# The splits of five token sums moved to later places in the order of ScalarE and VectorE

## The chip, the cores and the metric

The kernel runs on one core of a Trainium2 chip. The metric is the device time of one execution in microseconds (us): the median of several runs. TensorE (PE) does the matmuls, VectorE (DVE) and ScalarE (ACT) split operands and empty PSUM, GpSimd (POOL) adds, SyncE (SP) issues the DMAs.

## The reference

One encoder layer is applied to a prompt of 256 tokens and to a sample of 2048 tokens, both 1024 wide, in float32. What matters here is the first step, the projection of the normalised tokens by one weight matrix of 1024 x 3072:

```python
h = rms_norm(x, g_pre)
proj = h @ w_in
q, k, v, z_a, u_f, z_f = jnp.split(proj, [...], axis=-1)
y_a = neighbourhood_attention(q, k, v, rpb)
y_f = fourier_mix(u_f, w_fourier, b_fourier)
mixed = jnp.concatenate([rms_norm(y_a, g_na) * jax.nn.silu(z_a),
                         rms_norm(y_f, g_f) * jax.nn.silu(z_f)], axis=-1)
return x + rms_norm(mixed @ w_out, g_post)
```

## The kernel before, in words

**Three matmuls for one.** A float32 operand is held as two parts: a high part (a rounded copy, made by ScalarE) and a remainder (operand minus high part, made by VectorE). A product is high x high + high x remainder + remainder x high, so `mm3` (lines 170 to 173) issues three matmuls for each piece: L171, L172, L173. A product cannot pass its second or third matmul before the remainders are there.

**The prompt's stage** (lines 743 to 781) makes 16 blocks of the prompt's projections, numbered `b`. A block is 24 matmuls of 256 columns. `b_raw(b + 2)` (line 574) splits the weights of the block after next: ScalarE's cast `wh` (L577), VectorE's remainder `wl` (L578). ScalarE empties the block (L777) and SP stores it (L779, L781). Beside that, the stage makes work for the next one: `n_scale` scales the sample's tokens on VectorE (L416), `n_sum` forms sums and differences of token blocks on VectorE (L439, at b = 8 to 11), and `n_first(j)` (line 441) splits the j-th of seven such token operands: one ScalarE cast `xh` of 128 x 2048 (L444), one VectorE remainder `xl` of 128 x 2048 (L445). `op_split` (line 482) splits the weight operands `vh`, `vl` (L493, L494, for operand 5 L489, L490) in two halves each.

**The stage after it**, `vu(0, range(2, 4), hooks)` (lines 500 to 536, called in line 808), makes v and u of half of the sample's tokens by a scheme in which seven products of sums stand for eight. Its sequence has 14 steps, called products here, numbered i from 0: token operand 0 in steps 0 and 1, operand 1 in 2 and 3, and so on to operand 6 in 12 and 13. A product is 12 matmuls of 512 columns. At step i, before the matmuls, come in this order: loads of weight sums (`op_load`, SP), splits of weight sums (`op_split`: operand 2 at i = 2, 3 at 4, 4 at 6, 5 at 8, 6 at 10), and the functions hooked to i in the order in which they were hooked. Hooked are `n_first`, `rows_load(5)` to `rows_load(8)` (SP, line 298, at i = 1, 3, 5, 7; 1024 KB each, called xm5 to xm8 here), `rows_square` of these (ScalarE, two L305 activations with accumulators, at i = 4, 6, 8, 10), and from i = 8 on the first weights of the next stage (`w_load`, `w_sums`, `a_split`: L562, L563). After the matmuls of a product VectorE adds it up (L521; in products 0 and 1 ScalarE copies it, L524), and SP stores the finished ones (L364).

**What sets the order.** All engines but the DMA rings run in the order in which the code is written; no scheduler moves anything. Tiles of 8 KB a partition (`xh`, `xl`, `xm`, the sums) share 16 buffers, so a load waits for the last reader of the buffer that it gets.

Of the kernel before, what the change touches and what calls it, by code (L numbers as in the profile page):

```python
# [169 lines left out]
def mm3(nc, out, lh, ll, rh, rl, first, last):  # L170
    nc.tensor.matmul(out, lh, rh, start=first, stop=False)  # L171
    nc.tensor.matmul(out, lh, rl, start=False, stop=False)  # L172
    nc.tensor.matmul(out, ll, rh, start=False, stop=last)  # L173


def build(tc, A, O):
# [46 lines left out]
    def mmt(n):  # L223
        x = mmc[0] % 5 > 2
        mmc[0] += 1
        return ps.tile([128, n], F32, tag="t" if x else "a", name="mm", bufs=2 if x else 3)
# [21 lines left out]
    def k8(dtype, name, shape=(128, 4, 512)):  # L248
        return hp.tile(list(shape), dtype, tag="k8", name=name, bufs=NK)
# [151 lines left out]
    def n_load(x):  # L401
        if type(x) is tuple:
            nq[x] = k8(F32, "nx")
            nc.sync.dma_start(nq[x], A["xq"][0, x[0], x[1]])
            return
        nx = [k8(F32, "nx") for kh in range(2)]
        for kh in range(2):
            for b in range(2):
                nq[x, kh, b] = nx[kh][:, 2 * b:2 * b + 2]
                nc.sync.dma_start(nq[x, kh, b], A["xq"][1, kh, b][:, 2 * x:2 * x + 2])  # L410

    def n_scale(x, kh, b, ks=range(4)):
        v_ = nq[kh, b] if x is None else nq[x, kh, b]
        for k in ks if x is None else range(2):
            kk = 4 * kh + 2 * (x or 0) + k
            nc.vector.scalar_tensor_tensor(out=v_[:, k], in0=v_[:, k], scalar=gpre[:, kk:kk + 1],  # L416
                                           in1=ivp[int(x is not None)][b], op0=ALU.mult, op1=ALU.mult)
# [16 lines left out]
    def n_sum(x):  # L434
        if x == 0:
            nq["t3"] = k8(F32, "nt")
        o, i0, i1, op = (("t3", (1, 1), (0, 1), ALU.subtract), ((0, 1), (0, 1), (0, 0), ALU.subtract),
                         ((0, 0), "t3", (0, 0), ALU.add), ((1, 0), (0, 0), (1, 0), ALU.subtract))[x]
        nc.vector.tensor_tensor(out=nq[o], in0=nq[i0], in1=nq[i1], op=op)  # L439

    def n_first(j):
        src = nq[((0, 0), (1, 0), (0, 0), (0, 1), "t3", (1, 0), (1, 1))[j]]
        h, l = bnew[0, j] = [k8(F32R, "x" + x) for x in "hl"]
        nc.scalar.copy(h, src)  # L444
        nc.vector.tensor_tensor(out=l, in0=src, in1=f_(h), op=ALU.subtract)  # L445
# [27 lines left out]
    def op_load(j):  # L473
        if j < 2:
            l = [load(US, A["wv"][j][:, 2 * x:2 * x + 2], "vr") for x in range(2)]
        else:
            l = [gt(US, F32R, "vl") for x in range(2)]
            for x in range(2):
                nc.sync.dma_start(f_(l[x]), sD[(3, 2, 1, 0, 4)[j - 2]][:, 2 * x:2 * x + 2])
        op_[j] = [None, l]  # L480

    def op_split(j):
        r = op_[j][1]
        h = op_[j][0] = [gt(US, F32R, "vh"), hp.tile([128, 2, 512], F32R, tag="vw", name="vh", bufs=3)]
        l = op_[j][1] = [gt(US, F32R, "vl") for x in range(2)] if j < 2 else r
        for x in range(2):
            src = r[x] if j < 2 else f_(r[x])
            if j == 5:
                nc.scalar.activation(h[x], src, AF.Copy, scale=-1.0)  # L489
                nc.vector.scalar_tensor_tensor(out=l[x], in0=src, scalar=-1.0, in1=f_(h[x]), op0=ALU.mult,  # L490
                                               op1=ALU.subtract)
            else:
                nc.scalar.copy(h[x], src)  # L493
                nc.vector.tensor_tensor(out=l[x], in0=src, in1=f_(h[x]), op=ALU.subtract)  # L494
# [79 lines left out]
    def b_raw(b):  # L574
        wh, wl = [gt(BS, F32R, "w" + x) for x in "hl"]
        src = wp_[b]
        nc.scalar.copy(wh, src)  # L577
        nc.vector.tensor_tensor(out=wl, in0=src, in1=wh.bitcast(F32), op=ALU.subtract)  # L578
        wb[b] = wh, wl
# [106 lines left out]
    def wz_load(n):  # L686
        for x in range(n):
            wp_.append(load(BS, A["wz"][len(wp_)], "wr"))
# [54 lines left out]
    for b in range(16):  # L743
        kind, blk = divmod(b, 4)
        if b < 10:
            wz_load(1)
        if b in (0, 2):
            n_load((b // 2, 1))
        if b == 10:
            op_load(0)  # L750
        if b == 12:
            op_load(1)
        if b < 14:
            b_raw(b + 2)
        if b < 8:
            x, y = divmod(b, 2)
            n_scale(None, *divmod(x, 2)[::-1], range(2 * y, 2 * y + 2))
        elif b < 12:
            n_sum(b - 8)
        if b in (3, 5, 12, 13):  # L760
            n_first((3, 5, 12, 13).index(b))
        if b > 13:
            op_split(b - 14)
        p = mmt(512)[:, :TP]
        wh, wl = wb.pop(b)
        for k in range(KC):
            mm3(nc, p, wh[:, k], wl[:, k], hp_[:, k], lp_[:, k], k == 0, k == KC - 1)
        o = st.tile([128, 256], F32, tag="f", name="f", bufs=3)
        if kind == 1:
            v = [(o, p)]  # L770
        elif kind == 3:
            v = [(o[:, 128 * x:128 * x + 128].rearrange("p (x r c) -> p r x c", x=2, c=16),
                  p[:, 128 * x:128 * x + 128].rearrange("p (r x c) -> p r x c", x=2, c=16)) for x in range(2)]
        else:
            v = [(o.rearrange("p (r b c) -> p b r c", b=2, c=32), p.rearrange("p (b r c) -> p b r c", b=2, c=32))]
        for d, i in v:
            nc.scalar.activation(d, i, AF.Silu if kind < 2 else AF.Copy, scale=-0.125 if kind == 3 else 1.0)  # L777
        if kind < 2:
            nc.sync.dma_start(zD[kind, blk * 128:blk * 128 + 128, :TP], o)  # L779
        else:  # L780
            nc.sync.dma_start((kD if kind == 2 else qD)[blk, :, :TP], o)  # L781

    def call(f, *a):
        return lambda: f(*a)
# [11 lines left out]
    def at(i, f, *a):  # L796
        hooks.setdefault(i, []).append(call(f, *a))

    for x in range(4, 7):
        at(3 * x - 12, n_first, x)  # L800
    for x in range(4):
        at(2 * x + 1, rows_load, x + 5)
        at(2 * x + 4, rows_square, x + 5)
# [19 lines left out]
    for i in range(16):  # L823
# [48 lines left out]
        for j in range(7):  # L872
# [28 lines left out]
            if sg == 0:  # L901
                x, y = divmod(7 * (pr - 1) + j, 14)
# [19 lines left out]
            for f, d in ((u_load, 0), (u_split, 3), (u_stage1, 5)):  # L922
                x = 7 * pr + j - 7 - d
# [649 lines left out]
    for k in range(2, len(G) + 2):  # L1573
# [17 lines left out]
        x = k // 2  # L1591
# [68 lines left out]
        if 32 <= k < 36:  # L1660
            x, d = k - 32, atiles[k - 32]
# [126 lines left out]
```

## Time and profile before

| | |
|---|---|
| median of 3 runs | 938.73 us (937.64 to 939.05) |
| the profiled execution's own time | 937.48 us |
| its span, first to last instruction | 935.7 us |
| TensorE busy | 925.3 us, 99% |
| VectorE busy | 669.9 us, 72% |
| ScalarE busy | 469.8 us, 50% |
| granted TensorE clock | 0.999 |

The profiled execution took 937.48 us, of which 935.7 us lie between its first and its last instruction; all times below that are not a median are counted from the span's start. In the timeline's rows stand the start, the duration, the engine (a q behind it: its queue, for DMA issues), the line, the operation, the tiles written and read, the shape and how many were merged into the row; idle time of the engine ahead of it and what ended it stand in square brackets. A row that merges several starts with the first and ends with the last. Consecutive instructions of VectorE or ScalarE overlap by about 0.09 us, so the step from start to start says what one costs in a series.

### The profile page before, as it was taken

The page shows a single profiled execution, that of the slowest core. Times are in us where ns is not written, and L with a number is a line of the kernel's source. Part 1 is how long each engine was busy: PE and PEld are TensorE (multiplying, and loading weights), DVE is VectorE, ACT ScalarE, POOL GpSimd, SP SyncE. Part 2 cuts the span into 40 slices and gives each one's busy share as a digit, 9 for nine tenths or more (in the row PEclk, how much of TensorE's full clock was granted, in tenths as well). Part 3 has the DMA queues.
Part 4 walks back from the last instruction along what each step waited for, and adds up shares of the span by engine and source line. Part 5 has one row for each costly group of instructions (what it writes and reads, how often), then busy time and mean ns, then how long its engine had stood idle before and what let it go on. Part 6 is the DMA issues. An engine that isn't in the chain of part 4 may idle for free.

```text
span 935.7 us, 18895 instructions
## 1 busy us (share of the span) xinstructions
PE 925.3 (99%) x6790; PEld 774.5 (83%) x6790; DVE 669.9 (72%) x1308; ACT 469.8 (50%) x1038; POOL 332.0 (35%) x337
## 2 busy tenths in 40 slices
PE   9999999999999999999999999999999999999997
PEld 7889988888888888888888888978788887888886
DVE  6487997688864967597666645677665666659997
ACT  5856577623332743233334425667655666654443
POOL 3200002436650300363333200445456565525444
PEclk9999999999999999999999999999999999999999
DMA  9899777468573999758888789888779899879993
GB/s 323 329 360 400 217 253 281 158 246 314 201 288 151 352 400 359 265 209 316 294 310 286 273 287 309 295 262 257 245 248 274 264 300 283 255 237 377 341 340 128
DMA packets 144829, 264.04 MB, mean 282 GB/s; under 512 B 21784, under 2 KB 84632, under 8 KB 141984
## 3 DMA queue, kind: packets, MB, share of 16 engines
q1 hardware_dynamic: 144576, 262.81, 80.9%
q8 instruction: 54, 0.88, 0.4%
q14 instruction: 39, 0.32, 0.1%
q10 hardware_dynamic: 160, 0.02, 0.0%
HBM read 174.75 MB, written 95.35 MB: 289 GB/s over the span
## 4 chain that ended last, share of the span: by engine, by line
PE 94%; DMA 3%; DVE 2%; issue 1%; ACT 0%; DVEq 0%; SPq 0%
PE mm L172 18%; PE mm L173 18%; PE mm L171 17%; PE ptb L1425 10%; PE po L1425 10%; PE pv L1508 5%; PE ptb L1485 3%; PE s L1179 3%; PE pab L1005 2%; PE ptb L1179 2%; DMA woD<-wo 1%; PE py L171 1%; PE py L173 1%; PE py L172 1%; PE pf L1425 1%
## 5 line engine op out<-in xcount | busy, mean ns | idle before, releaser
L171 PE MATMUL mm<-xh,wa 128*128 128x512 f32 x448 | 174.4, 389 | 0.0
L173 PE MATMUL mm<-xh,wa 128*128 128x512 f32 x448 | 174.3, 389 | 0.0
L172 PE MATMUL mm<-xl,wa 128*128 128x512 f32 x448 | 174.3, 389 | 0.0
L548 POOL TENSOR_TENSOR ws<-wr 128x512 f32<-128x512 f32 x16 | 22.2, 1386 | 259.3 <-DMA wr<-wz 246.2
L171 PEld LDWEIGHTS mm<-xh,wa 128*128 128x128 f32 x448 | 84.1, 188 | 17.5
L173 PEld LDWEIGHTS mm<-xh,wa 128*128 128x128 f32 x448 | 84.1, 188 | 17.4
L172 PEld LDWEIGHTS mm<-xl,wa 128*128 128x128 f32 x448 | 84.1, 188 | 17.4
L1425 PE MATMUL po<-w,yh 128*128 128x512 f32 x280 | 86.8, 391 | 0.0
L1425 PE MATMUL ptb<-wo,yh 128*128 128x512 f32 x272 | 86.7, 400 | 0.0
L1213 POOL TENSOR_SCALAR w<-w,m 128x352 f32<-128x352 f32 (+4 forms) x136 | 75.4, 572 | 30.4 <-PE s L1179 14.0
L563 DVE TENSOR_TENSOR wa<-wr,wa 128x512 fp32r<-128x512 f32 x60 | 57.7, 969 | 30.6 <-ACT wa L562 30.3
L1206 ACT ACTIVATE w<-w,m 128x352 f32<-128x352 f32 (+4 forms) x136 | 69.9, 521 | 12.5 <-DVE m L1201 12.1
L861 DVE TENSOR_TENSOR f<-u,mm 128x512 f32<-128x512 f32 x64 | 43.6, 681 | 34.1 <-PE mm L173 29.5
L172 PE MATMUL mm<-vl,xh 128*128 128x512 f32 x168 | 65.6, 390 | 0.4 <-DVE vl L494 0.4
L171 PE MATMUL mm<-vh,xh 128*128 128x512 f32 x168 | 65.4, 389 | 0.0
L173 PE MATMUL mm<-vh,xl 128*128 128x512 f32 x168 | 65.4, 389 | 0.0
L1425 PEld LDWEIGHTS ptb<-wo,yh 128*128 128x128 f32 x272 | 49.3, 188 | 14.8 <-ACT sqa L1536 3.4
L1425 PEld LDWEIGHTS po<-w,yh 128*128 128x128 f32 x280 | 52.3, 188 | 11.0
L562 ACT CAST wa<-wr 128x512 fp32r<-128x512 f32 x60 | 36.5, 617 | 42.7 <-PE mm L173 16.8
L1508 PEld LDWEIGHTS pv<-pt,v 96*64 96x64 f32 (+2 forms) x1280 | 45.2, 137 | 11.6 <-issue 6.6
L1425 PE MATMUL po<-w,yl 128*128 128x512 f32 x140 | 54.5, 389 | 0.0
L1425 PE MATMUL ptb<-wo,yl 128*128 128x512 f32 x136 | 53.1, 391 | 0.0
(249 smaller groups left out, 2192.3 us busy)
## 6 DMA issues: line engine op xcount, KB each, us to landing
wr<-wz SPq DMA_DIRECT2D x48, 512.0 KB
vl<-sD SPq DMA_DIRECT2D x20, 512.0 KB
xm<-xm SPq DMA_DIRECT2D x9, 1024.0 KB
oD<-ofs SPq DMA_DIRECT2D x18, 512.0 KB
of<-oD SPq DMA_DIRECT2D x18, 512.0 KB
yr<-yD SPq DMA_DIRECT2D x34, 256.0 KB
zD<-f SPq DMA_DIRECT2D x16, 512.0 KB
woD<-wo SPq DMA_DIRECT2D x16, 512.0 KB
```

The lines of the kernel that those rows point to most:

```text
L171: nc.tensor.matmul(out, lh, rh, start=first, stop=False)
L172: nc.tensor.matmul(out, lh, rl, start=False, stop=False)
L173: nc.tensor.matmul(out, ll, rh, start=False, stop=last)
L562: nc.scalar.copy(o[:, 0], src)
L563: nc.vector.tensor_tensor(out=o[:, 1], in0=src, in1=o[:, 0].bitcast(F32), op=ALU.subtract)
L861: nc.vector.tensor_tensor(out=dst(f, b), in0=src(uu[u]), in1=src(p), op=op)
L1179: nc.tensor.matmul(sp[2 * b + h][64 * y:64 * y + 64, j * w:(j + n) * w], g["q"][hs, 128 * b + 64 * y:128 * b + 64 * y + 64], kk[hs, k:k + ...
L1206: nc.scalar.activation(w, w, AF.Exp, bias=m[:, h:h + 1], scale=-1.0, accum_out=m[:, 2 + h:3 + h])
L1213: nc.gpsimd.tensor_scalar(w, w, m[:, 4 + h:5 + h], 1.0, ALU.mult, ALU.mult)
L1425: nc.tensor.matmul(p, (d["l"] if x == 2 else d["h"])[:, c], w(n, int(x == 1), c), start=j == 0, stop=j == 11)
L1485: nc.tensor.transpose(ptb[2 * b + y][:nk, x:x + 64], g["w"][b][ys, h, c0:c0 + nk], ident[ys, ys])
L1508: nc.tensor.matmul(p[hs, b, o], v[:nk, b, x, hs], g["pt"][b][:nk, h, j * 128 + o.start:j * 128 + o.stop], start=first, stop=last)
```

## The change

Two lists of numbers that set when `n_first` is called are changed; nothing else:

```diff
@@ in the loop over b @@
-        if b in (3, 5, 12, 13):
-            n_first((3, 5, 12, 13).index(b))
+        if b in (3, 5, 13):
+            n_first((3, 5, 13).index(b))
@@ ahead of vu(0, ...) @@
-    for x in range(4, 7):
-        at(3 * x - 12, n_first, x)
+    for x in range(3, 7):
+        at(3 * x - 8 if x > 3 else 1, n_first, x)
```

Operand 2 is split at b = 13 instead of 12, operand 3 at product 1 instead of b = 13, operands 4, 5 and 6 at products 4, 7 and 10 instead of 0, 3 and 6. Each keeps its cast on ScalarE and its remainder on VectorE. The instructions of TensorE, GpSimd and SP stand as before; some of the shared buffers change hands.

In the rows below, names carry the number of the tile in the program. The remainders `xl` of operands 2 to 6 are xl_1193, xl_1230, xl_1345, xl_1407 and xl_1481 before, and xl_1226, xl_1356, xl_1431, xl_1494 and xl_1567 now; `wl` are the remainders of a block's weights (the last three belong to blocks 13, 14 and 15), `vl` those of weight sums, two for an operand.

VectorE before, from block 11 to the start of the products:

```order
L578 TENSOR_TENSOR wl_1152<-wr_1007,wh_1151 128x1024
L439 TENSOR_TENSOR nx_677<-nx_594,nx_677 128x2048
L578 TENSOR_TENSOR wl_1189<-wr_1043,wh_1188 128x1024
L445 TENSOR_TENSOR xl_1193<-nx_594,xh_1192 128x2048
L578 TENSOR_TENSOR wl_1226<-wr_1079,wh_1225 128x1024
L445 TENSOR_TENSOR xl_1230<-nx_745,xh_1229 128x2048
L494 TENSOR_TENSOR vl_1264<-vr_1114,vh_1262 128x1024
L494 TENSOR_TENSOR vl_1265<-vr_1116,vh_1263 128x1024
L494 TENSOR_TENSOR vl_1301<-vr_1184,vh_1299 128x1024
L494 TENSOR_TENSOR vl_1302<-vr_1186,vh_1300 128x1024
L445 TENSOR_TENSOR xl_1345<-nt_1049,xh_1344 128x2048
```

The same stretch of VectorE now:

```order
L578 TENSOR_TENSOR wl_1152<-wr_1007,wh_1151 128x1024
L439 TENSOR_TENSOR nx_677<-nx_594,nx_677 128x2048
L578 TENSOR_TENSOR wl_1189<-wr_1043,wh_1188 128x1024
L578 TENSOR_TENSOR wl_1222<-wr_1079,wh_1221 128x1024
L445 TENSOR_TENSOR xl_1226<-nx_594,xh_1225 128x2048
L494 TENSOR_TENSOR vl_1260<-vr_1114,vh_1258 128x1024
L494 TENSOR_TENSOR vl_1261<-vr_1116,vh_1259 128x1024
L494 TENSOR_TENSOR vl_1297<-vr_1184,vh_1295 128x1024
L494 TENSOR_TENSOR vl_1298<-vr_1186,vh_1296 128x1024
L445 TENSOR_TENSOR xl_1356<-nx_745,xh_1355 128x2048
```

The weights of block 15 stand one long remainder earlier, the first weight sums too.

ScalarE before, products 4 to 10 (xm_1363, xm_1410, xm_1454 and xm_1501 are xm5 to xm8; vh_1474 and vh_1475 belong to operand 4, vh_1518 and vh_1519 to 5, vh_1564 and vh_1565 to 6; xh_1480 is the cast of token operand 6):

```order
L305 ACTIVATE xm_1363,ssq_108<-xm_1363 128x1024 x2
L493 CAST vh_1474<-vl_1402 128x1024
L493 CAST vh_1475<-vl_1403 128x1024
L444 CAST xh_1480<-nx_819 128x2048
L305 ACTIVATE xm_1410,ssq_108<-xm_1410 128x1024 x2
L489 ACTIVATE vh_1518<-vl_1428 128x1024
L489 ACTIVATE vh_1519<-vl_1429 128x1024
L305 ACTIVATE xm_1454,ssq_108<-xm_1454 128x1024 x2
L493 CAST vh_1564<-vl_1470 128x1024
L493 CAST vh_1565<-vl_1471 128x1024
L305 ACTIVATE xm_1501,ssq_108<-xm_1501 128x1024 x2
```

The same stretch of ScalarE now (xm_1359, xm_1402, xm_1450 and xm_1497 are xm5 to xm8; xh_1493 and xh_1566 are the casts of token operands 5 and 6):

```order
L305 ACTIVATE xm_1359,ssq_108<-xm_1359 128x1024 x2
L493 CAST vh_1470<-vl_1398 128x1024
L493 CAST vh_1471<-vl_1399 128x1024
L305 ACTIVATE xm_1402,ssq_108<-xm_1402 128x1024 x2
L444 CAST xh_1493<-nx_677 128x2048
L489 ACTIVATE vh_1514<-vl_1420 128x1024
L489 ACTIVATE vh_1515<-vl_1421 128x1024
L305 ACTIVATE xm_1450,ssq_108<-xm_1450 128x1024 x2
L493 CAST vh_1560<-vl_1466 128x1024
L493 CAST vh_1561<-vl_1467 128x1024
L444 CAST xh_1566<-nx_819 128x2048
L305 ACTIVATE xm_1497,ssq_108<-xm_1497 128x1024 x2
```

The cast of token operand 6 stood ahead of the squares of xm6 and now stands behind those of xm7; that of operand 5 (before it stood ahead of this piece, at product 3) now stands behind the squares of xm6.

VectorE before, from the second half of weight operand 4 to that of weight operand 6 (`u4`, `uc` and `vuo` are the sums after products 6 to 9):

```order
L494 TENSOR_TENSOR vl_1403<-vl_1403,vh_1475 128x1024
L445 TENSOR_TENSOR xl_1481<-nx_819,xh_1480 128x2048
L521 TENSOR_TENSOR u4_1499<-uc_1361,mm_1486 128x512
L521 TENSOR_TENSOR u4_1516<-uc_1378,mm_1503 128x512
L490 SCALAR_TENSOR_TENSOR vl_1428<-vl_1428,vh_1518 128x1024
L490 SCALAR_TENSOR_TENSOR vl_1429<-vl_1429,vh_1519 128x1024
L521 TENSOR_TENSOR vuo_1543<-u4_1499,mm_1530 128x512
L521 TENSOR_TENSOR uc_1361<-uc_1361,mm_1530 128x512
L521 TENSOR_TENSOR vuo_1560<-u4_1516,mm_1547 128x512
L521 TENSOR_TENSOR uc_1378<-uc_1378,mm_1547 128x512
L494 TENSOR_TENSOR vl_1470<-vl_1470,vh_1564 128x1024
L494 TENSOR_TENSOR vl_1471<-vl_1471,vh_1565 128x1024
```

The same stretch of VectorE now:

```order
L521 TENSOR_TENSOR u4_1491<-uc_1353,mm_1478 128x512
L445 TENSOR_TENSOR xl_1494<-nx_677,xh_1493 128x2048
L521 TENSOR_TENSOR u4_1512<-uc_1374,mm_1499 128x512
L490 SCALAR_TENSOR_TENSOR vl_1420<-vl_1420,vh_1514 128x1024
L490 SCALAR_TENSOR_TENSOR vl_1421<-vl_1421,vh_1515 128x1024
L521 TENSOR_TENSOR vuo_1539<-u4_1491,mm_1526 128x512
L521 TENSOR_TENSOR uc_1353<-uc_1353,mm_1526 128x512
L521 TENSOR_TENSOR vuo_1556<-u4_1512,mm_1543 128x512
L521 TENSOR_TENSOR uc_1374<-uc_1374,mm_1543 128x512
L494 TENSOR_TENSOR vl_1466<-vl_1466,vh_1560 128x1024
L494 TENSOR_TENSOR vl_1467<-vl_1467,vh_1561 128x1024
L445 TENSOR_TENSOR xl_1567<-nx_819,xh_1566 128x2048
```

The remainder of token operand 6 stood ahead of eleven rows of this piece and now ends it; in its old place, one sum later, stands that of operand 5.

## The prediction

> **What bounds the kernel now.** I read the page first, then TensorE's waits, then the timelines of the four queues around the change.
>
> ```profile
> PE 925.3 (99%) x6790; PEld 774.5 (83%) x6790; DVE 669.9 (72%) x1308; ACT 469.8 (50%) x1038; POOL 332.0 (35%) x337
> ...
> PEclk9999999999999999999999999999999999999999
> PE hot L604 <- POOL onesq L232: 1.0, 1, 1.0
> PE mm L173 <- DVE wl L578: 0.8, 4, 0.2
> ...
> PE ptb L1485 <- DVE m L1201: 0.4, 1, 0.4
> PE mm L172 <- DVE vl L494: 0.4, 2, 0.2
> ```
>
> TensorE is busy 99% of the span, so only what makes it pause, or ends a pause, moves the end. The list of its waits (in all, times, longest) is short: the four for `wl` and one of the two for `vl` are in the prompt's stage and right behind it. TensorE's timeline shows what one costs (start, duration):
>
> ```profile
> 115.43 0.39 PE L173 MATMUL mm<-ph,wl 128*128 128x256 f32 x1 [0.21 <-DVE wl L578]
> ...
> 118.29 0.28 PE L172 MATMUL mm<-pl,wh 128*128 128x256 f32 x1
> 118.77 0.39 PE L173 MATMUL mm<-ph,wl 128*128 128x256 f32 x1 [0.20 <-DVE wl L578]
> 118.99 0.28 PE L171 MATMUL mm<-ph,wh 128*128 128x256 f32 x1
> 119.11 0.28 PE L172 MATMUL mm<-pl,wh 128*128 128x256 f32 x1
> ...
> 121.50 0.39 PE L171 MATMUL mm<-vh,xh 128*128 128x512 f32 x1
> 122.11 0.50 PE L172 MATMUL mm<-vl,xh 128*128 128x512 f32 x1 [0.21 <-DVE vl L494]
> 122.44 0.39 PE L173 MATMUL mm<-vh,xl 128*128 128x512 f32 x1
> ...
> 160.10 0.39 PE L171 MATMUL mm<-xh,wa 128*128 128x512 f32 x1
> ```
>
> The 0.2 us in brackets is not the price. From start to start a short matmul takes 0.12 us; across the pause at 118.77 it is 0.48, and the next step is 0.22 instead of 0.12. So a pause here costs 0.36 + 0.10 = 0.46 us; at 122.11 it is 0.61 and 0.33 against 0.227 (below), again about 0.48. Behind 122.44 the 14 products run without a pause to 160.10: 166 steps of (160.10 - 122.44) / 166 = 0.227 us, 2.722 a product.
>
> VectorE's timeline shows why the pauses come:
>
> ```profile
> 110.80 1.24 DVE L578 TENSOR_TENSOR wl<-wr,wh 128x1024 fp32r<-128x1024 f32 x1
> ...
> 114.14 1.24 DVE L578 TENSOR_TENSOR wl<-wr,wh 128x1024 fp32r<-128x1024 f32 x1
> 115.27 2.31 DVE L445 TENSOR_TENSOR xl<-nx,xh 128x2048 fp32r<-128x2048 f32 x1
> 117.47 1.24 DVE L578 TENSOR_TENSOR wl<-wr,wh 128x1024 fp32r<-128x1024 f32 x1
> 118.61 2.31 DVE L445 TENSOR_TENSOR xl<-nx,xh 128x2048 fp32r<-128x2048 f32 x1
> 120.81 4.65 DVE L494 TENSOR_TENSOR vl<-vr,vh 128x1024 fp32r<-128x1024 f32 x4
> ```
>
> A block's `wl` (1.13) and a long pass (2.20) make 3.33 us a block, while TensorE needs 24 x 0.12 = 2.88. VectorE is the later one, and TensorE waits at each block.
>
> **Part one: the two remainders ahead of the products.** Up to the `wl` at 114.14 nothing changes, so the pause at 115.43 stays. The next `wl` moves from 117.47 to 115.27, ready at 116.5; operand 2's remainder follows at 116.40, the first `vl` at 118.60, ready at 119.8. TensorE reaches block 15's third matmul at 115.43 + 0.22 + 23 x 0.12 = 118.41, product 0 at 118.41 + 22 x 0.12 = 121.05 and its third matmul at 121.50: both operands are there, no pause. Against 122.44 that is 0.94 us gained. Operand 2's remainder is needed in product 4, operand 3's in product 6 (138 us): covered.
>
> **Part two: operands 5 and 6, behind the row squares.** Product i now has its third matmul, the first that reads `xl`, at 121.50 + 2.722 i: product 10 at 148.72, product 12 at 154.16. When are their remainders made? On ScalarE the cast of operand 5 now stands behind the squares of xm6, and these wait for a DMA. The rows of before: ScalarE, one of VectorE, SP, and the DMAs' share and GB/s by stretch (the last two numbers of the two last rows):
>
> ```profile
> 124.94 0.59 ACT L524 COPY uc<-mm 128x512 f32<-128x512 f32 x1 [0.94 <-PE mm L173]
> ...
> 140.06 1.91 ACT L444 CAST xh<-nx 128x2048 fp32r<-128x2048 f32 x1
> 141.88 1.05 ACT L305 ACTIVATE xm<-xm 128x1024 f32<-128x1024 f32 x1
> ...
> 143.97 2.00 ACT L489 ACTIVATE vh<-vl 128x1024 fp32r<-128x1024 f32 x2
> 147.40 1.06 ACT L305 ACTIVATE xm<-xm 128x1024 f32<-128x1024 f32 x1 [1.44 <-DMA xm<-xm]
> ...
> 152.49 1.06 ACT L305 ACTIVATE xm<-xm 128x1024 f32<-128x1024 f32 x1 [1.01 <-DMA xm<-xm]
> ...
> 131.50 0.68 DVE L521 TENSOR_TENSOR vuo<-uc,mm 128x512 f32<-128x512 f32 x1
> ...
> 132.21 0.32 SPq L364 DMA_DIRECT2D vN<-vuo  x1
> 132.58 0.92 SPq L479 DMA_DIRECT2D vl<-sD x2
> 133.60 0.38 SPq L300 DMA_DIRECT2D xm<-xm  x1
> ...
> 146.42 0.38 SPq L300 DMA_DIRECT2D xm<-xm  x1
> 131.50:136.50 5.00, 5.00 (x23) 4.13 (x23) 5.00 (x6) 4.36 (x6) 0.00 (x0) 1.00 0.89 274
> 136.50:147.40 10.90, 10.90 (x49) 9.01 (x48) 7.62 (x8) 8.09 (x12) 0.00 (x0) 1.00 1.02 408
> ```
>
> xm7 ended ScalarE's wait at 147.40. Between it and xm6 a 256 KB store, two 512 KB loads and xm7's own 1024 KB passed, 2.36 MB at the 408 GB/s of the last row: 5.8 us, so xm6 landed at about 141.6 (an estimate; it is hidden, ScalarE was busy until 141.88). Now: block 15 ends 0.46 us earlier, and with it SP's run of loads starts. The store at 132.21, behind which xm6 is issued, waits for the sum of 131.50 on VectorE (three rows behind the first piece of the order shown). That sum now stands behind operand 3's remainder: product 0 ends at 121.05 + 2.72 = 123.77, its copy starts 0.23 later as before (124.94 against 124.71), 0.5 for the copy and 1.9 for the cast make 126.4, the remainder and two `vl` 2.2 + 2.27, the sum 0.68: 131.6 instead of 132.2. I take xm6 at 0.5 us earlier, 141.1; the bounds are no earlier (141.6) and twice that (140.6).
>
> From there: squares 2.09 (141.88 to 143.97), cast 1.91, a hop between engines of 0.05 (117.47 + 1.24 to 118.77): operand 5's remainder starts at 145.15. VectorE then has an unbroken series. Its rows of before give each step:
>
> ```profile
> 144.10 2.29 DVE L445 TENSOR_TENSOR xl<-nx,xh 128x2048 fp32r<-128x2048 f32 x1 [2.60 <-ACT xm L305]
> 146.31 1.28 DVE L521 TENSOR_TENSOR u<-uc,mm 128x512 f32<-128x512 f32 x2
> 147.50 2.36 DVE L490 SCALAR_TENSOR_TENSOR vl<-vl,vh 128x1024 fp32r<-128x1024 f32 x2
> 149.77 0.68 DVE L521 TENSOR_TENSOR vuo<-u,mm 128x512 f32<-128x512 f32 x1
> ...
> 152.16 2.36 DVE L494 TENSOR_TENSOR vl<-vl,vh 128x1024 fp32r<-128x1024 f32 x2
> 154.43 0.68 DVE L521 TENSOR_TENSOR vuo<-uc,mm 128x512 f32<-128x512 f32 x1
> ```
>
> Remainder 5: 2.21; one sum: 0.60; weight operand 5: 2.27; four sums: 2.39; weight operand 6: 2.27; remainder 6: 2.29. Together 12.03, so operand 6's remainder is ready at 157.18. ScalarE doesn't hold this series: from 145.1 it needs 1.9 for weight operand 5, 2.1 for the squares of xm7 (landed by 147), 1.9 and 1.9 for the casts of operand 6, done at 152.9, and VectorE comes to that remainder only at 154.9. Those 2.0 us are cover.
>
> TensorE meets it twice. Product 10's second matmul (148.50) wants the first half of weight operand 5, ready at 145.15 + 2.21 + 0.60 + 1.22 = 149.18: a pause of 0.7. Product 12's third matmul then waits to 157.23, where it would have stood at 154.16. The first pause lies inside the second sum, since the second ends at a fixed time. With a restart of 0.11 and 22 steps of 0.227 the next stage starts at 157.23 + 0.11 + 4.99 = 162.33 instead of 160.10: **2.23 us later** (+3.17 of pauses, -0.94 of part one). Bounds by xm6's landing: 2.7 and 1.7.
>
> Past 160 us nothing gives it back: of TensorE's waits only the 0.4 for `m` lies there. The first weights of the next stage are also split later on VectorE, by about 158.5, and are wanted at 162.3. Moved past xm6 and xm7 are only a cast and a remainder each, no DMA; xm8 gets another buffer, whose last reader is the squares of xm6 instead of remainder 6, so it and the two weight loads behind it on SP are issued about 3 us earlier than at 146.42.
>
> That last point meets a rule. In the rows xm8, issued at 146.42, landed 5.1 us behind xm7: the time of its own 1024 KB and of the 1024 KB of weight sums issued ahead of it, at 408 GB/s, so loads landed in the order of issue. The Trainium skill, DMA: Bandwidth & Descriptors, section Queues, rings and completion order, says that each DMA engine takes descriptors in ring order, but that completion is not first in, first out. By ring order the earlier loads change nothing in the sum; if they shared the rate with xm7 and weight operand 6, up to 2 MB or 5.1 us would be pushed ahead, 2.0 of it covered, and the sum would grow by up to 3.1. The rows speak for order, and I leave it out.
>
> **How the numbers follow.** The profiled execution's 937.48 becomes 939.7. The median lies 1.25 above that execution, inside the spread of the runs, so I add to the median: 938.73 + 2.2 = **940.9**. A measurement of this kernel can tell about 0.2%, 1.9 us, from no change.
>
> - **Forecast, 0.72:** two late pauses, +1.7 to +2.7.
> - **Half of it, 0.15:** xm6 lands clearly earlier. Between 131.5 and 136.5 the DMAs moved 274 GB/s where 408 were to be had; if the earlier issue wins all of that, 0.67 MB or 1.6 us, operand 6 is ready at 155.6 and the change costs 0.6; I put the case at +0.6 to +1.6, 939.8. Against it: the store that holds SP back moves by 0.6 only.
> - **The gain stands, 0.06:** no late pause, 938.73 - 0.94 = 937.8, not slower. It needs operand 6's remainder by 154.1, xm6 by 138.0; the change breaks even at 138.9. Nothing in the rows brings the load 2.2 us forward.
> - **The clock drops, 0.07:** the pauses of 0.7 and 2.3 us are longer than any of before (1.0 at most, granted clock 0.999 throughout), so none of its rows shows what follows. If the next matmuls ran at half pace for as long as the pause lasted, that adds 1.1: 942.0. The Trainium skill, TensorE: Matmul & The Clock Gate, section What's actually happening, lets the clock fall only after an idle window of about 3.4 us and rise after as much work; by it these pauses do nothing, and if it did fall, half pace for one window would add 1.7, 942.6.
>
> The range of 939.0 to 942.4 holds the forecast with its bounds and a scatter of the runs of 0.7, most of the half case and the clock's. Slower by over 0.2% (above 940.6): about 0.72 of the forecast's cases and the clock's, 0.60. Faster by over 0.2% needs the gain and luck: 0.03. Within: 0.37.
>
> **What would show it.** Right: no wait for `wl` behind 115.5 and none for `vl` at product 0; product 0 near 121.05; a wait of TensorE for `vl` L490 near 149 and one of about 2 us for `xl` L445 near 157, the following stage at about 162.3; remainder 5 on VectorE starting near 145 on the end of its cast, behind the squares of xm6. Wrong: remainder 6 done before 154, or a landing of xm6 ahead of 139; or steps above 0.23 us behind the long pause, which would be the clock.

## The result and the profile after

The changed kernel takes 943.16 us, median of 11 runs (939.83 to 945.78), where the kernel before takes 938.43 (937.64 to 940.37, 11 runs): a ratio of 1.0049, 95% interval 1.0036 to 1.0062, so it is 0.36 to 0.62% slower. The forecast was 940.9, with a range up to 942.4: the sign is right, the size is not. Its profiled execution (939.83 us, span 938.0) is the fastest of the eleven.

The list of TensorE's waits (in all, times, longest) reads as forecast. Of the waits for `wl` those of blocks 13 and 14 are left (the one at 97 us in before is missing by chance: a second execution of the changed kernel, below, has it at 98.88), none is for `vl` L494; two new ones stand in the products, the longer one at the head of the list:

```profile
PE mm L173 <- DVE xl L445: 3.1, 1, 3.1
...
PE mm L172 <- DVE vl L490: 0.8, 1, 0.8
PE mm L173 <- DVE wl L578: 0.4, 2, 0.2
```

TensorE's timeline of the changed kernel, from block 13's pause to the next stage's first matmul:

```profile
111.29 0.39 PE L173 MATMUL mm<-ph,wl 128*128 128x256 f32 x1 [0.21 <-DVE wl L578]
...
120.25 0.40 PE L171 MATMUL mm<-vh,xh 128*128 128x512 f32 x1
...
148.65 0.50 PE L172 MATMUL mm<-vl,xh 128*128 128x512 f32 x1 [0.79 <-DVE vl L490]
...
157.73 0.50 PE L173 MATMUL mm<-vh,xl 128*128 128x512 f32 x1 [3.12 <-DVE xl L445]
...
162.85 0.39 PE L171 MATMUL mm<-xh,wa 128*128 128x512 f32 x1
```

This execution reached block 13 0.80 us earlier than that of before (111.29 against 112.09), by chance: nothing that TensorE waits for up to there was moved. So the stretch from block 13's pause to the next stage is the one to compare: 162.85 - 111.29 = 51.56, against 160.10 - 112.09 = 48.01. The change costs 3.55 here, 1.3 more than the 2.23 of the forecast. Its rows on ScalarE, VectorE and GpSimd show where:

```profile
140.54 1.06 ACT L305 ACTIVATE xm<-xm 128x1024 f32<-128x1024 f32 x1 [1.46 <-DMA xm<-xm]
142.64 1.90 ACT L444 CAST xh<-nx 128x2048 fp32r<-128x2048 f32 x1
```

```profile
144.57 2.29 DVE L445 TENSOR_TENSOR xl<-nx,xh 128x2048 fp32r<-128x2048 f32 x1 [3.64 <-ACT xh L444]
...
152.04 2.35 DVE L494 TENSOR_TENSOR vl<-vl,vh 128x1024 fp32r<-128x1024 f32 x2
154.31 3.37 DVE L445 TENSOR_TENSOR xl<-nx,xh 128x2048 fp32r<-128x2048 f32 x1
```

```profile
154.24 1.28 POOL L548 TENSOR_TENSOR ws<-wr 128x512 f32<-128x512 f32 x1 [126.50 <-PE mm L173]
155.60 3.22 POOL L548 TENSOR_TENSOR ws<-ws,wr 128x512 f32<-128x512 f32 x1
```

The chain is the forecast's: xm6 lands, its squares, operand 5's cast, an unbroken series on VectorE, operand 6's remainder. Against block 13, xm6 landed at 140.54 - 111.29 = 29.25 (where the squares end a wait for it, their start stands for the landing), and the forecast had 141.1 - 112.09 = 29.0. And the last remainder took 3.37 us instead of 2.29. GpSimd's first sum of the next stage's weights (L548) had started 0.07 us ahead of it and ended at 155.52; from there the remainder's own 2.29 leads to 157.8 (its row ends at 157.68), and GpSimd's second sum, started at 155.60, ends at 158.82, about one sum behind that. The two did not slow each other down by halves: one stood while the other ran.

### The profile page after: what moved, and what is told of

Same layout as the page of the kernel before. It is cut to its first block, busy times and chain, and to the rows that moved or that the text cites. A ratio compares the mean times of both kernels' runs of the same rounds, so it can differ in the third digit from the quotient of the medians.

```text
span 938.0 us, 18890 instructions
## 1 busy us (share of the span) xinstructions
PE 925.1 (99%) x6790; PEld 774.5 (83%) x6790; DVE 668.5 (71%) x1308; ACT 469.7 (50%) x1038; POOL 333.0 (36%) x337
## 4 chain that ended last, share of the span: by engine, by line
PE 93%; DMA 3%; DVE 2%; issue 1%; ACT 0%; SPq 0%; DVEq 0%
PE mm L173 17%; PE mm L172 17%; PE mm L171 17%; PE ptb L1425 10%; PE po L1425 10%; PE pv L1508 5%; PE ptb L1485 3%; PE s L1179 2%; PE pab L1005 2%; PE ptb L1179 2%; DMA wr<-wz 1%; PE py L171 1%; PE py L173 1%; PE py L172 1%; DMA xm<-xm 1%
## 5 line engine op out<-in xcount | busy, mean ns | idle before, releaser
L548 POOL TENSOR_TENSOR ws<-wr 128x512 f32<-128x512 f32 x16 | 21.1, 1319 | 261.2 <-PE mm L173 133.8
```

## The experiments

The theory after the result: the end of the products hangs on one chain, from xm6's landing over ScalarE's order to operand 6's remainder, lengthened by 1.08 where a sum on GpSimd goes first. Its rivals: the clock, which read 0.996 in nine of the eleven runs of the changed kernel (0.998 in the profiled one); and a cost of the first part. The diffs are against the changed kernel, unless said otherwise.

**Operands 2 and 3 alone moved.**

```diff
-        at(3 * x - 8 if x > 3 else 1, n_first, x)
+        at(3 * x - 12 if x > 3 else 1, n_first, x)
```

> The kernel after, with the splits of operands 4 to 6 back at products 0, 3 and 6; only those of operands 2 and 3 stay moved. My theory: the loss sits wholly in operands 5 and 6, and the two small pauses at block 15 and product 0 are a gain of its own, so this is about 0.9 us faster than before (937.5 where before has 938.4), with TensorE's waits for wl at two instead of four, none for vl L494 at product 0, no wait of over 0.5 us for xl or vl later, and the mean clock of before (0.998 or 0.999). Rival, the loss comes from somewhere else in the change (operand 3's late split): then this kernel is as slow as after, 942 to 943.

Measured: 938.67 (937.02 to 941.02), ratio 1.0006 (0.9996 to 1.0015): the loss is gone, but the gain of 0.94 did not come. From block 13's pause to the next stage it took 162.21 - 114.06 = 48.15, 0.14 more than before. The two pauses are gone; TensorE stops at product 10 instead, for a step of 1.18 instead of 0.227 and 0.11 behind it:

```profile
151.43 0.50 PE L172 MATMUL mm<-vl,xh 128*128 128x512 f32 x1 [0.79 <-DVE vl L490]
```

```profile
146.75 2.29 DVE L445 TENSOR_TENSOR xl<-nx,xh 128x2048 fp32r<-128x2048 f32 x1 [2.67 <-ACT xm L305]
...
150.16 2.36 DVE L490 SCALAR_TENSOR_TENSOR vl<-vl,vh 128x1024 fp32r<-128x1024 f32 x2
```

On VectorE weight operand 5 (L490) stands behind operand 6's remainder, and that waited for the squares of xm6 (the row names them). In before this place has 0.7 us to spare: the first half of weight operand 5 is there at 147.50 + 1.22 = 148.72, and its matmul starts at 149.44. Here TensorE came 0.94 us earlier, and L490 started 36.10 us behind block 13's pause instead of 35.41. Why the remainder waits for squares that it doesn't read is not shown.

**Operands 4 to 6 alone moved** (against before).

```diff
     for x in range(4, 7):
-        at(3 * x - 12, n_first, x)
+        at(3 * x - 8, n_first, x)
```

> The kernel before, with only the splits of operands 4 to 6 at products 4, 7 and 10. My theory: all of the loss is here, and without the gain of the first part it is larger than after by about 0.9 us: pauses of about 0.5 at product 10 and 3 at product 12, the last remainder stretched beyond 2.3 us beside GpSimd's weight sums, and in the runs without the profiler a mean clock of 0.996: some 943.5 to 944.5. Rival, the two parts only harm together (the work that part one pushes behind product 0 delays the rest): then this one stands at 940 or below.

Measured: 943.05 (941.57 to 943.93), ratio 1.0044 (1.0032 to 1.0056). The whole loss is here. It is not larger than that of the changed kernel, so part one gives nothing back there either: the end follows the landing of xm6, not TensorE's arrival. Rows of ScalarE and VectorE, GpSimd, TensorE:

```profile
143.07 1.06 ACT L305 ACTIVATE xm<-xm 128x1024 f32<-128x1024 f32 x1 [1.50 <-DMA xm<-xm]
```

```profile
156.84 2.29 DVE L445 TENSOR_TENSOR xl<-nx,xh 128x2048 fp32r<-128x2048 f32 x1
```

```profile
156.86 3.41 POOL L548 TENSOR_TENSOR ws<-wr 128x512 f32<-128x512 f32 x1 [127.86 <-PE mm L173]
```

```profile
159.18 0.50 PE L173 MATMUL mm<-vh,xl 128*128 128x512 f32 x1 [2.03 <-DVE xl L445]
...
164.30 0.39 PE L171 MATMUL mm<-xh,wa 128*128 128x512 f32 x1
```

Here VectorE started first, by 0.02 us (GpSimd's spans in the profile are rough): the remainder took 2.29, and GpSimd's sum 3.41 instead of 1.28. From the landing to the next stage: 164.30 - 143.07 = 21.23 us, to the digit the forecast's 162.33 - 141.1. In the changed kernel it was 162.85 - 140.54 = 22.31, the 1.08 of the held-up remainder more.

**The next stage's weights loaded two products later.**

```diff
-    at(8, w_load, 0)
+    at(10, w_load, 0)
```

> The kernel after, with the next stage's first weight load at product 10 instead of 8, so that GpSimd's weight sums start later than the last remainder. My theory, in which that remainder took 3.37 us because GpSimd's sums ran beside it: it takes 2.3 to 2.6 again, TensorE's pause at product 12 falls from 3.1 to about 2.1, the next stage starts about 1 us earlier, and, if the clock falls only after a pause of some 3 us, the mean clock returns to 0.998 and the time to 940 to 941. Rival, the remainder is slow for another reason (ScalarE's or the DMAs' work beside it): it still takes over 3 us and the time stays at 943. A later load could itself make the next stage wait for its weights, which the list of waits would show.

Measured: 942.77 (940.63 to 944.27), ratio 1.0041 (1.0028 to 1.0055). GpSimd's first sum started at 161.86, behind the last remainder, which took 2.29:

```profile
145.11 1.06 ACT L305 ACTIVATE xm<-xm 128x1024 f32<-128x1024 f32 x1 [1.47 <-DMA xm<-xm]
```

```profile
158.87 2.29 DVE L445 TENSOR_TENSOR xl<-nx,xh 128x2048 fp32r<-128x2048 f32 x1
```

```profile
166.35 0.39 PE L171 MATMUL mm<-xh,wa 128*128 128x512 f32 x1
```

166.35 - 145.11 = 21.24: without the sum the chain has its plain length. This execution was no faster all the same, because in it xm6 landed 30.42 us behind block 13's pause (114.69) instead of 29.25. So the held-up remainder was a part of the loss, and the landing is another. The median fell by 0.4 us only, which is inside the scatter; where xm6 landed in the runs that weren't profiled is not known.

**Dummy matmuls in the pauses.** The first kernel has ten at product 12, the second four at product 10 and twelve at product 12; they are added work on constants, and nothing reads their result.

```diff
+    def fill(n):
+        p = ps.tile([128, 128], F32, tag="c", name="fill", bufs=1)
+        for i in range(n):
+            nc.tensor.matmul(p, onesq, onesq, start=True, stop=True)
+
+    at(10, fill, 4)
+    at(12, fill, 12)
```

> The kernel after, with ten added 128x128 matmuls on constants ahead of product 12's own, whose result nobody reads: TensorE has work in most of the long pause. My theory, by which the pause makes the clock fall in the runs without the profiler: the next stage starts where it does in after, within 0.3 us, the mean clock is 0.998 instead of 0.996, and the time is 1 to 2.5 us below after, 940.5 to 942. Rival, the clock's lower mean comes from elsewhere, or the time beyond the pause comes from the DMAs: clock and time stay as in after, 943.

> The kernel after, with dummy matmuls on constants ahead of product 10 (4 of them) and of product 12 (12), whose result nobody reads, so that TensorE doesn't stop for over 1 us in the products. If the clock is what after loses beyond its pauses, the mean clock is 0.998 or 0.999 in nearly all runs, no step of 0.43 stands in the products, and the time is 1 to 2 us below that of after in the same series. Rival: the clock is restored and the time is not, within 0.7 us of after, as in the kernel with ten such matmuls (943.3 against 943.2): then the clock is not what after loses, and the rest is spread over the first stage.

Measured: 943.30 (941.47 to 946.59), mean clock 0.997 to 0.999, and 944.04 (942.46 to 944.86), 0.997 to 0.998: the clock is mostly back, the time is not (1.0050 and 1.0060 of before, intervals within 1.0034 to 1.0073). The second expectation's rival holds; of the first's rival the time holds, the clock doesn't. TensorE's rows of the first (the row counts each of the ten twice): it works through the pause and reaches the next stage no sooner than the chain lets it:

```profile
158.57 2.39 PE L811 MATMUL fill<-onesq 128*128 128x128 f32 x20
160.72 0.48 PE L171 MATMUL mm<-vh,xh 128*128 128x512 f32 x1
...
166.34 0.39 PE L171 MATMUL mm<-xh,wa 128*128 128x512 f32 x1
```

xm6's squares began at 145.10 there: again 21.24 to the next stage. In the second it is 164.45 - 142.86 = 21.59; its dummies held product 12 back until 158.92, so that TensorE came to the remainder a little late.

**The changed kernel again.**

> The kernel after, unchanged, for a second profiled execution: its first one had a mean clock of 0.998, nine of its ten other runs 0.996. If the clock falls in those behind the pauses of the products, a profiled execution at 0.996 shows steps of 0.43 instead of 0.227 us for some 3.4 us behind product 10 or 12 (16 steps, +1.7 us), as the kernel with operand 5 alone late showed behind a pause of 2.5, and the products then take over 43 us. Rival, the clock is lost elsewhere, in the first stage: then steps of 0.43 stand at 8 to 12 us only, and the products take the 42.6 us of the first profile or less.

Measured: 943.78 (943.49 to 945.78), ratio to before in this series 1.0059 (1.0046 to 1.0072). In this execution the clock did fall, from 1.5 us behind the pause at product 10 on. TensorE's rows, and a stretch of half pace with the granted clock (0.54), the DMAs' share and GB/s:

```profile
152.25 0.50 PE L172 MATMUL mm<-vl,xh 128*128 128x512 f32 x1 [1.89 <-DVE vl L490]
...
154.54 0.63 PE L171 MATMUL mm<-vh,xh 128*128 128x512 f32 x1
154.97 0.63 PE L172 MATMUL mm<-vl,xh 128*128 128x512 f32 x1
...
161.35 0.50 PE L173 MATMUL mm<-vh,xl 128*128 128x512 f32 x1 [1.50 <-DVE xl L445]
...
166.47 0.39 PE L171 MATMUL mm<-xh,wa 128*128 128x512 f32 x1
```

```profile
154.00:157.50 3.50, 3.50 (x10) 0.54 0.75 297
```

Seven steps took 0.43 instead of 0.227, and the two beside them a part of that, 1.6 us in all (not the sixteen steps of the expectation: 3.4 us hold eight of 0.43), and the pause at product 12 was that much shorter (1.50 instead of 3.12): TensorE came late to something that was later still. The end is again the chain's: xm6's squares began at 144.15, 166.47 - 144.15 = 22.32, with GpSimd's sum in front once more (157.70 to 159.16, the remainder 157.91 to 161.30). The rest of the difference to the first execution is the landing, 144.15 - 113.80 = 30.35 behind block 13's pause.

**One late operand at a time.** Operands 2 and 3 as in the changed kernel; first operand 5 alone late (at 7), then operand 6 alone (at 10).

```diff
-        at(3 * x - 8 if x > 3 else 1, n_first, x)
+        at({3: 1, 4: 0, 5: 7, 6: 6}[x], n_first, x)
```

> Operands 2 and 3 moved as in after, operand 4 at product 0, operand 5 alone late, at product 7, and operand 6 at product 6 as in before. If the pauses of after have their own cause each (operand 5's remainder that at product 10, operand 6's that at product 12), this one has only a pause of 1 to 1.2 at product 10, and stands 0 to 0.5 above before, 938.6 to 939.1. Rival, operand 5's late remainder pushes all that follows on VectorE, so that product 12 waits as well: 2 us or more above before, 941.

> Operands 2 and 3 moved as in after, operand 4 at product 0, operand 5 at product 3 as in before, and operand 6 alone late, at product 10. If operand 6's place alone makes the long pause at product 12 (its cast behind the squares of xm7 and the casts of weight operand 6, its remainder behind four sums and those of weight operand 6), the wait for xl L445 is 2 to 3 us and the time 941. Rival, the long pause needs operand 5's late start as well: the wait is about 1 us, the next stage starts within 0.3 us of before, and the time is 938.4 to 939.

Measured, operand 5 late: 941.07 (939.75 to 945.34), 1.0029 (1.0015 to 1.0043). The rival's time, but not its mechanism: product 12 doesn't wait. There is one pause, at product 10, as first expected, but of 2.45, since both long remainders now stand ahead of weight operand 5 on VectorE (143.91 and 147.94, L490 at 150.75); and behind it the clock at half pace, which counts here, as no later wait swallows it:

```profile
152.02 0.58 PE L172 MATMUL mm<-vl,xh 128*128 128x512 f32 x1 [2.45 <-DVE vl L490]
152.40 0.63 PE L173 MATMUL mm<-vh,xl 128*128 128x512 f32 x1
152.82 0.63 PE L171 MATMUL mm<-vh,xh 128*128 128x512 f32 x1
...
155.77 0.40 PE L172 MATMUL mm<-vl,xh 128*128 128x512 f32 x1
```

Operand 6 late: 939.47 (937.80 to 941.93), 1.0008 (0.9998 to 1.0019); waits of 0.57 for `xh` and 1.59 for `xl` at product 12. The time is nearer to the rival's, but the next stage started 162.05 - 112.26 = 49.79 us behind block 13's pause, 1.78 later than in before, where the rival had at most 0.3. So operand 6's place alone makes a part of the late start; all of it needs operand 5's late start as well.

**The squares behind the casts.**

```diff
-        at(2 * x + 4, rows_square, x + 5)
+        at(2 * x + 5 + 2 * (x == 2), rows_square, x + 5)
```

> The kernel after, with the row squares of xm6 and xm7 one and three products later, behind the casts of operands 5 and 6 on ScalarE. If the late remainders come from the casts' place behind squares that wait for a landing, operand 5's remainder starts some 2 us earlier against block 13, the pause at product 10 vanishes and the long one shrinks to about 1. Rival, by VectorE's own order: the first pause vanishes, but operand 6's remainder still stands behind the four sums and the two passes of weight operand 6, whose loads land when they land, so the wait for xl L445 stays at 2 to 2.5 us and the products take some 41 us; the time falls by 0.6 to 1.5 against after.

Measured: 943.06 (940.32 to 943.45), 1.0042 (1.0029 to 1.0056). The pause at product 10 is gone, the long one is 3.11, and the products take 162.91 - 121.40 = 41.51. This is the rival's outcome, with a longer wait than its 2 to 2.5 and by another step: the remainder waited for squares in this order too, although its cast was done at 153.33. ScalarE, then VectorE:

```profile
151.43 1.90 ACT L444 CAST xh<-nx 128x2048 fp32r<-128x2048 f32 x1
```

```profile
155.45 2.29 DVE L445 TENSOR_TENSOR xl<-nx,xh 128x2048 fp32r<-128x2048 f32 x1 [2.67 <-ACT xm L305]
```

**xm6 asked for at product 1.**

```diff
-        at(2 * x + 1, rows_load, x + 5)
+        at(2 * x + 1 if x != 1 else 1, rows_load, x + 5)
```

> The kernel after, with xm6's load asked for at product 1, right behind xm5's, so that SP issues it ahead of the store that it waited behind, into a stretch where the DMAs had room. In six profiled executions of kernels with the late operands the next stage started 21.23 to 21.6 us behind the landing of xm6, or 22.3 where a sum on GpSimd held up the last remainder, whatever that landing was. If that landing sets the end, it moves by several us and the squares of xm6 no longer wait for it, but follow weight operand 4's casts: operand 5's remainder starts some 31.8 us behind block 13's pause instead of 33.3 (34.4 in the second execution of after), the pause at product 10 goes, the products take 41 to 41.7 us instead of 42.6 to 43.7, and the time is 1 to 2 us below after, 941.5 to 942.5. Rival, the loads' total rate sets it, so that the earlier load only pushes weight operand 4's back: products of 42.5 us or more, 943 to 944.

Measured: 947.05 (945.28 to 948.69), 1.0092 (1.0074 to 1.0111), the slowest of all. The rival holds, and more: behind the load that went ahead, weight operand 4's landed later, and the casts of that stand ahead of the squares on ScalarE. ScalarE, VectorE, TensorE:

```profile
141.62 1.05 ACT L493 CAST vh<-vl 128x1024 fp32r<-128x1024 f32 x1 [3.71 <-DMA vl<-sD]
142.90 1.05 ACT L493 CAST vh<-vl 128x1024 fp32r<-128x1024 f32 x1 [0.23 <-DMA vl<-sD]
143.86 1.05 ACT L305 ACTIVATE xm<-xm 128x1024 f32<-128x1024 f32 x1
```

```profile
155.35 3.46 DVE L494 TENSOR_TENSOR vl<-vl,vh 128x1024 fp32r<-128x1024 f32 x2
158.73 3.36 DVE L445 TENSOR_TENSOR xl<-nx,xh 128x2048 fp32r<-128x2048 f32 x1
```

```profile
163.99 0.63 PE L173 MATMUL mm<-vh,xl 128*128 128x512 f32 x1
...
168.90 0.39 PE L171 MATMUL mm<-xh,wa 128*128 128x512 f32 x1
```

From the squares to the next stage 168.90 - 143.86 = 25.04. That is the chain's 21.23, twice a pass held up by a sum on GpSimd (3.46 for 2.36, 3.36 for 2.29: 2.2), and steps of 0.43 behind the last pause, 1.6.

**Operand 6 one product earlier, and then two of the sums as well.** Against the kernel with operands 2 and 3 alone moved, the first puts operand 6's split at product 5 instead of 6; the second also moves two of VectorE's four sums of token blocks.

```diff
-        at(3 * x - 12 if x > 3 else 1, n_first, x)
+        at({3: 1, 4: 0, 5: 3, 6: 5}[x], n_first, x)
... the second also
-        elif b < 12:
-            n_sum(b - 8)
+        elif b in (8, 9, 11):
+            n_sum(min(b - 8, 2))
+    at(0, n_sum, 3)
```

> The kernel with only operands 2 and 3 moved, and operand 6's split one product earlier, at 5 instead of 6: its cast stands ahead of weight operand 4's and of the squares of xm6 on ScalarE. Without that last edit the kernel lost its 0.94 us again in a pause of 1.05 at product 10, whose weight operand stood on VectorE behind operand 6's remainder, and that remainder behind the squares of xm6. My theory now: the gain of part one is real but needs that chain to be early; with the cast ahead of the squares there is no wait for vl L490, the next stage starts 47.1 us behind block 13's pause instead of 48.0, and the time is 0.9 below before, 937.7. Rival, the chain that ends at product 10 is set by the loads alone (weight operand 5's landing): the pause of about 1 us stays and the time is that of before, 938.6.

> The kernel before it in this list, and two of the four token sums moved as well: the third from block 10 to 11, the fourth from block 11 to product 0, so that VectorE has no two long passes in blocks next to each other. My theory: all four pauses of 0.47 at blocks 13 to 15 and product 0 are gone and nothing replaces them, the next stage starts about 1.9 us earlier than in before (46.1 us behind block 13's third matmul), 936.8. Rival, as for that kernel, a later step that hangs on the loads takes the gain back: 938 to 939, with a new wait in the products.

Measured, the first: 937.27 (936.13 to 938.69), ratio to before 0.9986 (0.9977 to 0.9994); no wait for `vl` L490, and 159.46 - 112.39 = 47.07 from block 13's pause to the next stage, as expected. The second: 935.37 (934.61 to 937.46), ratio 0.9970 (0.9959 to 0.9981), faster than the kernels before and after, by 1.8 to 3.8 us against before. Of its waits one for `wl` is left, at 98.96, ahead of all that was moved. The next stage starts 160.01 - 113.51 = 46.50 us behind block 13's third matmul, where 46.1 was expected: of block 13's own pause only the 0.1 of its restart lies behind that matmul. The products take 160.01 - 121.91 = 38.10, which is 14 x 2.722 without any pause:

```profile
PE hot L604 <- POOL onesq L232: 1.0, 1, 1.0
PE mm L173 <- DVE wl L578: 0.9, 1, 0.9
PE py L1259 <- DVE w L1063: 0.7, 1, 0.7
PE mm L171 <- ACT wc L261: 0.3, 1, 0.3
```

## Why the prediction was wrong in size

**Part one, two pauses less: right in place, wrong as a gain.** The waits vanished as described. But alone it is worth nothing (1.0006): the sum looked at the pauses and not at the next place without slack, weight operand 5 at product 10, which had 0.7 us to spare. With operand 6's split moved out of that place's way the gain is there (0.9986).

**Part two, the mechanism: right.** The casts behind the squares, the unbroken series on VectorE, both pauses and their operands are as forecast, and so is the length of the chain: 21.23 from xm6's landing to the next stage, measured 21.23 and twice 21.24 in three other kernels with the same late operands, whose landings differ by 1.3 us.

**The first step that failed: "I take xm6 at 0.5 us earlier, 141.1".** That is 29.0 us behind block 13's pause, with bounds of 28.5 and 29.5. The two profiled executions of the changed kernel had 29.25 and 30.35. SP did not issue the load 0.5 us earlier: it did so 21.42 and 21.40 us behind that pause, and in before 133.60 - 112.09 = 21.51. SP's rows, of the first execution and of the second:

```profile
132.71 0.43 SPq L300 DMA_DIRECT2D xm<-xm  x1
```

```profile
135.20 0.43 SPq L300 DMA_DIRECT2D xm<-xm  x1
```

What went wrong there is "the remainder and two `vl` 2.2 + 2.27": the second of these `vl` waited for its cast, and the cast for a load of weight sums, so that the sum behind it, and the store that SP issues ahead of xm6, came as late as before. ScalarE and VectorE in the first execution (the second has the same two waits, 0.95 and 0.45):

```profile
128.44 1.05 ACT L493 CAST vh<-vl 128x1024 fp32r<-128x1024 f32 x1 [0.99 <-DMA vl<-sD]
```

```profile
129.53 1.23 DVE L494 TENSOR_TENSOR vl<-vl,vh 128x1024 fp32r<-128x1024 f32 x1 [0.48 <-ACT vh L493]
```

The rest is the time from issue to landing, in the forecast 141.6 - 133.60 = 8.0, measured 7.8 and 9.0. The estimate took a bound from one execution for a bound over executions: in six other kernels that have block 13's pause and whose squares of xm6 end a wait for the load, it landed 29.10 to 30.64 us behind that pause.

**The second: "remainder 6: 2.29".** The series was added up from VectorE's rows alone. In both profiled executions of the changed kernel a sum on GpSimd started just ahead of that remainder, by 0.07 and 0.21 us, and the remainder took 3.37 and 3.39. The forecast saw the weight loads behind that sum go out earlier, but weighed them only as DMA traffic ("I leave it out"). They did go out earlier, by 2.9 and 1.8 us, but the sum hardly did: it started 42.95 and 43.90 us behind block 13's pause, and in before 43.73. It is the remainder that moved, from 32.01 to 43.02 and 44.11, into the sum's time. Tenths decide who is first: with operands 4 to 6 alone moved, and in both kernels with dummy matmuls, the remainder was, by 0.02 to 0.31 us, and took 2.28 to 2.29. The kernel with a later load, whose sum comes after the remainder, has 2.29 as well.

The two make the sum: 2.23 + 0.24 + 1.08 = 3.55 for the first execution, as measured; 2.23 + 1.34 + 1.09 = 4.66 for the second, measured 166.47 - 113.80 - 48.01 = 4.66. The median is 4.7 and 5.4 us above before in the two series, somewhat more than these stretches; what the other runs had isn't in a trace. A single execution's total says less: the first block began at 73.1 to 77.3 us in the profiled executions, though nothing ahead of it was changed in any kernel. That the runs of the changed kernel spread over 5.9 us and those of before over 2.7 fits the landing, which lies on the path only after the change; it wasn't shown run by run.

**The rival "the clock drops" (0.07): it happens, and cost nothing in the profile of the changed kernel that has it.** Half pace came behind pauses of 1.89 and 2.45 us, and with xm6 early behind 2.19 and 2.62, while pauses of 1.94, 2.02, 2.03, 3.11 and 3.12 us in other executions went by without it. The forecast cited the Trainium skill, TensorE: Matmul & The Clock Gate, section What's actually happening, for an idle window of about 3.4 us; all four pauses are shorter than that, and the measurement decides. Where another wait follows, the price is nil, as the second execution of the changed kernel shows, and the kernels with dummy matmuls agree (clock back, time not); where no wait follows it was 1.6 (xm6 early, behind the last pause, and operand 5 alone late). A mean clock doesn't say where it fell: the profiled execution with operands 2 and 3 alone moved reads 0.996, and its half pace stands between 5 and 15 us, in the first stage. Whether the changed kernel's unprofiled runs lose some of that behind product 12 stays open; neither of its two profiles shows it there.

**The other rivals.** Half of the loss and the standing gain both needed an earlier landing, and no profile of the changed order shows one.

## What to carry to other kernels

When a moved step puts a transfer's landing on the path, count the rest of the path from that landing, and take the landing's bounds from several executions, not one. On the way to that landing, ask of each pass what load its operand waits for: a step that starts earlier in the order need not start earlier in time. Look on GpSimd for work that a moved VectorE pass now meets; who starts first can hang on tenths of a microsecond. A pause taken away is worth what the next place without slack leaves of it, so look for that place before counting the gain.

## What the hardware showed that was not expected

- **VectorE and GpSimd took turns.** A VectorE subtraction of two tiles and a GpSimd addition of two tiles did not share: the one that started later lasted until the other had ended, and then its own time (remainder 3.37 for 2.29 behind a sum of 1.28; sum 3.41 for 1.28 behind a remainder of 2.29, with starts 0.07 and 0.02 us apart). The Trainium skill, SBUF — State Buffer, section SBUF: two separate sides, says this of the port pair that the two share, for a VectorE instruction with two inputs in SBUF and a GpSimd one that reads SBUF: whichever starts first holds the pair for the whole instruction, and the other is blocked. These rows agree.
- **The clock fell behind shorter pauses than thought**, 1.89 us at the shortest, and not behind every longer one (3.12). It did not always fall at once: with operand 5 alone late half pace began with the first matmul, in the second execution of the changed kernel 1.5 us later. It came back after some 3.4 us of steps of 0.43.
- **A load issued earlier pushed back one behind it.** With xm6 asked for at product 1, weight operand 4's second half was there 29.8 us behind block 13's pause (142.90), instead of 26.7 and 27.9 in the two executions of the changed kernel (138.02 and 141.68), and from 127 us to 152 the DMAs had next to no room. Stretches with the granted clock, the DMAs' share and GB/s:

```profile
127.00:132.00 5.00, 5.00 (x23) 1.00 1.02 397
...
147.00:152.00 5.00, 2.81 (x14) 1.00 1.02 407
```
